# Modulation products on four column strips, two pairs' exponent bounds on the other engine, and an update rate without its sigmoid

## The chip, the cores and the metric

The kernel runs on one core of a Trainium2 chip. The metric is device time in microseconds of one execution; of several runs the median is taken. A profiled execution gives the trace from which all durations below come.

## The reference, cut to what matters

Two transformer layers work on 256 context tokens and 512 latent tokens of width 1024. The first layer's mixer is a gated delta rule ("GDN") with 8 key heads and 16 value heads, run forwards and backwards over the tokens; the second is a retention. The change touches only the beginning of the first layer.

```python
ml = [m[:, None, :] for m in adaln(c, w_mod[i], b_mod[i])]     # silu(c) @ w + b, six parts of 1024
mc = adaln(c_ctx, w_mod[i], b_mod[i])
hl = modulate(rmsnorm(xl, norm_mix_g[i]), ml[0], ml[1])        # h * (1 + scale) + shift
hc = modulate(rmsnorm(xc, norm_mix_g[i]), mc[0], mc[1])
...
# gdn_mixer
proj = jnp.concatenate([hc, hl], axis=1) @ w_in                # q, k, v, z, and ab: the gates
qkv = silu(short_conv(qkv, conv_w))
g = -jnp.exp(a_log) * softplus(ab[..., 0] + dt_bias)
beta = jax.nn.sigmoid(ab[..., 1])
...
# per head and chunk, G = cumsum(g)
seg = G[..., :, None] - G[..., None, :]
dec = jnp.where(incl, jnp.exp(jnp.where(incl, seg, 0.0)), 0.0)
a = jnp.where(strict, (k @ k.T) * dec * beta[..., :, None], 0.0)
sol = triangular_solve(a + I, rhs)                             # then the scan over chunks
```

## The kernel before, in words

The kernel is written in Python generators that emit instructions, and a scheduler that works with priorities (`tc.high_priority`) and a cost model of its own sets the order on each engine from them. Each engine then runs its instructions strictly in that written order, and so does the DMA queue of SyncE (SP in the rows), which issues nearly all loads. A change of a few instructions is therefore dealt out anew over the whole first mixer.

The start, `layer0_mix`, has three pieces that overlap.

- The modulation, `mod_cols`. Eight slices `mraw` of `w_mod` (1 MB each: scale and shift, four column blocks q of 256) are loaded. `cst` holds silu(c) and silu(c_ctx) as columns, 8 K-blocks of two vectors. For each slice eight products with a 128x2 stationary operand accumulate a 2x256 result `mps` (L146); each float32 product stands as two matmul records in the trace. ScalarE copies it to `mrow` (L148), two transposes turn it into columns `mtps` (L151), and VectorE adds bias and gain into `vec` (L155, L159).
- The tokens, `x_tile`. Six tiles of 128 tokens are loaded, normalised (L260, L262, L310) and transposed into `xraw` (L314, then L317 on ScalarE and L319 on VectorE).
- `mod_apply` turns `xraw` with `vec` into the two parts `xt` (a rounded high part, L172 on ScalarE, and a low part, L174 and L177 on VectorE), which all later projections read. A projection of one weight tile (`gemm_pair`, L91) is 24 products `gl` over the 512 latent tokens and 24 products `gc` over the context; its weights `raw` are split into `hl` by L56 (ScalarE) and L57 (VectorE).

Then `gdn_globals` computes the gates. The first projection is that of the ab columns (weights loaded by the eight small DMAs of L484). From its result come the update rate in rows 64 to 127 of `gb` (L510) and, through `xa`, Abs, Exp, Ln (L511 to L518), the log decay, whose running sum is made by two scans (L524, L526), stored to DRAM as `gd`, and brought back along the rows (`gtps` L542, `lbps` L550 turn them into columns). Behind it in program order come the conv projections of pair 0 (`conv_tile`: L579 on ScalarE and L582 on VectorE, then Silu L592, L595).

Heads are worked on in eight pairs. `gdn_bt(p)` loads the running sum along rows, broadcast to 128 partitions, as `e` (L645; 12 blocks of 128 for each direction), makes from each block relu(G_c - e), which bounds the exponent (L649), and later exp of its negative with a bias (L657). `gdn_s2(p)` multiplies masks and products with these (L673, L679, L682), and then runs a forward elimination of 30 steps on VectorE in which each step is a product `tmp` (L717) and a sum into `u` (L720) that the next step reads. After that the inverse is finished by small matmuls `ivps` (L754 and on) once VectorE has transposed the blocks (L745, L747), and the scan over chunks (`kk`, `uo`) begins. Between all this, projections of later pairs and gate tiles `zs` (L442) fill TensorE.

Of the kernel before, what the change touches and what calls it, by code (L numbers as in the profile page):

```python
# [10 lines left out]
F32 = mybir.dt.float32  # L11
# [31 lines left out]
class Trunk:  # L43
# [91 lines left out]
    def mod_cols(self, mp, pps, tags, col, xr):  # L135
        nc = self.nc
        vec = mp.tile([128, 2, 8, 2], F32, name="vec")
        for q in range(4):
            for ch in (1, 0):
                raw = mp.tile([128, 8, 256], F32, tag="mraw", name="mraw", bufs=4)  # L140
                c0 = ch * D + q * 256
                nc.sync.dma_start(
                    out=raw, in_=self.i["w_mod"][0, :, c0:c0 + 256].rearrange("(k p) f -> p k f", p=128))
                pr = pps.tile([2, 256], F32, tag=tags[ch], name="mps")
                for k in range(8):
                    nc.tensor.matmul(pr, lhsT=self.cst[:, k:16:8], rhs=raw[:, k], start=(k == 0), stop=(k == 7))  # L146
                row = mp.tile([2, 256], F32, tag="mrow", name="mrow", bufs=2)
                nc.scalar.activation(out=row, in_=pr, func=AF.Copy)  # L148
                ps = pps.tile([128, 2, 2], F32, tag="pp", name="mtps")
                for j in range(2):  # L150
                    nc.tensor.transpose(ps[:, j], row[:, j * 128:(j + 1) * 128], self.ident[0:2, 0:2])  # L151
                for j in range(2):
                    k = 2 * q + j
                    if ch:
                        nc.vector.tensor_scalar(  # L155
                            out=vec[:, 1, k], in0=ps[:, j], scalar1=col[:, 1, k:k + 1], scalar2=col[:, 2, k:k + 1],
                            op0=ALU.add, op1=ALU.mult)
                    else:
                        nc.vector.tensor_scalar(  # L159
                            out=vec[:, 0, k], in0=ps[:, j], scalar1=col[:, 0, k:k + 1], scalar2=None, op0=ALU.add)  # L160
                yield
            if q:
                self.mod_apply(vec, q - 1, xr)
# [125 lines left out]
    def layer0_mix(self):  # L289
# [58 lines left out]
        for _ in s1[0]:  # L348
            pass
        self.gdn_bt(0, st[0], prep)  # L350
        n = 0
        while True:
            with hi():
                if next(s2[0], 0) == 0:
# [3 lines left out]
                    self.gdn_kn(1, st[0], psk, scan)  # L358
                    self.gdn_bt(1, st[1], prep)
                    break  # L360
# [84 lines left out]
    def gdn_globals(self, keep, psk):  # L445
# [12 lines left out]
        with ExitStack() as es:  # L458
# [50 lines left out]
            for ps, t0, n in segs:  # L509
                nc.scalar.activation(out=gb[64:128, t0:t0 + n], in_=ps[64:128], func=AF.Sigmoid)  # L510
                nc.vector.tensor_scalar(  # L511
# [6 lines left out]
            nc.vector.scalar_tensor_tensor(out=xa, in0=xa, scalar=0.0, in1=e, op0=ALU.max, op1=ALU.add)  # L518
            nc.vector.tensor_scalar(out=xa[0:64], in0=xa[0:64], scalar1=na, scalar2=None, op0=ALU.mult)
            cm = gp.tile([64, T], F32, name="cm")  # L520
            nc.vector.memset(cm, 1.0)
# [109 lines left out]

    def gdn_bt(self, p, st, prep):
        nc = self.nc
# [8 lines left out]
        for d in range(2):  # L642
            e = prep.tile([128, 2 * NCH, CH], F32, tag=f"e{d}", name=f"e{d}")
            for h in range(2):
# [3 lines left out]
                for c in range(NCH):  # L648
                    nc.scalar.activation(  # L649
                        out=e[:, h * NCH + c], in_=e[:, h * NCH + c], func=AF.Relu, scale=-1.0,  # L650
                        bias=self.gs[:, d, 2 * p + h, c:c + 1])
            bt.append(e)
        for d in range(2):
            e = bt[d]
            for h in range(2):
                for c in range(NCH):
                    nc.scalar.activation(  # L657
                        out=e[:, h * NCH + c], in_=e[:, h * NCH + c], func=AF.Exp, scale=-1.0,
                        bias=lw[:, d, h, c:c + 1])
# [718 lines left out]
```

## Time and profile before

| | us |
|---|---|
| median of 3 runs | 2585.04 |
| lowest and highest | 2581.28, 2586.94 |
| the profiled execution | 2573.84 |
| its span in the trace | 2572.1 |
| TensorE busy in the span | 2431.1 (95%) |
| VectorE, ScalarE, GpSimd busy | 1667.7, 1073.5, 221.7 |

The profiled execution ran 11.2 us below the median, so sums are made against 2573.84 and then set on the median. TensorE is busy nearly throughout; the places where it is not are in the first mixer, which lasts until about 930 us. In the rows PE is TensorE's matmuls, PEld its weight loads, DVE VectorE, ACT ScalarE, POOL GpSimd, SPq the queue of SyncE. In brackets stands how long an engine was idle ahead of a row and what ended that.

### The profile page before, as it was taken

How to read it: one execution, taken by the hardware profiler on the slowest of the kernel's cores; microseconds unless marked ns; L12 is line 12 of the kernel's file. 1: busy time of each engine (PE TensorE's matmuls, PEld its weight loads, DVE VectorE, ACT ScalarE, POOL GpSimd, SP SyncE). 2: the span in 40 equal slices, each digit the busy share in tenths (PEclk: the TensorE clock that was granted, in tenths of full speed). 3: DMA queues.
4: the chain of work that ended last, by engine and by line, in shares of the span. 5: the costliest groups of instructions: out<-in, count | busy, mean ns of one | idle time of the engine just before them, and what ended most of it. 6: DMA issues, size and time to landing. Idle time of an engine off the chain costs nothing.

```text
span 2572.1 us, 39043 instructions
## 1 busy us (share of the span) xinstructions
PE 2431.1 (95%) x14879; PEld 2008.7 (78%) x14879; DVE 1667.7 (65%) x3362; ACT 1073.5 (42%) x2357; POOL 221.7 (9%) x268
## 2 busy tenths in 40 slices
PE   8799798998898999999999998999999999999998
PEld 4687686786777788778888887878888887788887
DVE  5568767787776755887776668874353546644446
ACT  5575555574555553253222221653231322532222
POOL 1102111111101110200000002000000002000001
PEclk9899899999899999999999999999999999999999
DMA  6332423423232247354443444243132223432332
GB/s 214 89 96 73 110 63 97 113 72 101 69 87 72 73 145 229 122 180 127 139 143 119 130 132 124 84 134 94 50 83 61 78 66 113 148 100 90 107 90 90
DMA packets 346827, 276.94 MB, mean 108 GB/s; under 512 B 105608, under 2 KB 293488, under 8 KB 346640
## 3 DMA queue, kind: packets, MB, share of 16 engines
q1 hardware_dynamic: 345616, 271.30, 35.4%
q10 hardware_dynamic: 1024, 3.15, 0.5%
q8 instruction: 117, 1.92, 0.3%
q14 instruction: 70, 0.57, 0.1%
HBM read 241.72 MB, written 32.67 MB: 107 GB/s over the span
## 4 chain that ended last, share of the span: by engine, by line
PE 55%; DVE 7%; DMA 3%; issue 2%; ACT 2%; POOL 0%; SPq 0%; POOLq 0%; ACTq 0%; DVEq 0%
PE pn L940 21%; PE gl L91 13%; PE rvp L1257 5%; PE gc L91 3%; PE rl L91 3%; PE rgp L1257 3%; PE pv L1287 2%; PE sc L1265 1%; DVE hl L57 1%; DVE ma L199 1%; PE rc L91 1%; DMA mraw<-in_w_mod 1%; ACT hl L56 0%; DVE o0acc L976 0%; DMA raw<-in_gdn_w_out 0%
## 5 line engine op out<-in xcount | busy, mean ns | idle before, releaser
L91 PE MATMUL gl<-xt,hl 128*128 128x512 f32 (+2 forms) x2760 | 700.8, 403 | 51.7 <-DVE acc L582 31.6
L91 PEld LDWEIGHTS gl<-xt,hl 128*128 128x128 f32 x2760 | 514.9, 193 | 160.0 <-issue 27.3
L57 DVE TENSOR_TENSOR hl<-raw,hl 128x1024 fp32r<-128x1024 f32 (+1 forms) x306 | 329.2, 1078 | 226.7 <-ACT hl L56 225.6
L940 PE MATMUL pn<-hl,fh 128*128 128x512 f32 x1920 | 445.0, 391 | 2.0 <-DVE fh L1074 1.9
L56 ACT ACTIVATE hl<-raw 128x1024 fp32r<-128x1024 f32 (+1 forms) x306 | 280.1, 920 | 396.9 <-PE pn L940 263.0
L940 PEld LDWEIGHTS pn<-hl,fh 128*128 128x128 f32 x1920 | 357.1, 188 | 80.1 <-DVE fh L1074 5.1
L91 PE MATMUL gc<-xt,hl 128*128 128x256 f32 x1944 | 274.8, 290 | 9.4 <-DVE acc L582 4.7
L91 PEld LDWEIGHTS gc<-xt,hl 128*128 128x128 f32 x1944 | 254.4, 194 | 20.6 <-ACT zs L442 5.4
L199 DVE SCALAR_TENSOR_TENSOR ma<-mraw,cst,ma 128x256 f32<-128x256 f32 x280 | 127.6, 496 | 40.0 <-DMA mraw<-in_w_mod 37.7
L940 PE MATMUL pn<-hl,yh 128*128 128x512 f32 x576 | 137.4, 397 | 5.4 <-DVE yh L57 4.1
L954 DVE TENSOR_TENSOR facc<-pn,facc 128x512 f32<-128x512 f32 x120 | 82.5, 689 | 83.1 <-PE pn L940 82.7
L1257 PE MATMUL rvp<-hl,xt 128*128 128x512 f32 x576 | 133.3, 390 | 0.6 <-DVE hl L57 0.6
L940 PEld LDWEIGHTS pn<-hl,yh 128*128 128x128 f32 x576 | 108.4, 191 | 31.2 <-DVE yh L57 5.8
L1257 PEld LDWEIGHTS rvp<-hl,xt 128*128 128x128 f32 x576 | 107.7, 188 | 23.5 <-DVE hl L57 1.1
L1071 ACT ACTIVATE fr<-gl 128x512 f32<-128x512 f32 x64 | 38.2, 597 | 202.1 <-PE gl L91 202.1
L582 DVE SCALAR_TENSOR_TENSOR acc<-gl,cw,acc 128x511 f32<-128x511 f32 (+1 forms) x96 | 71.5, 745 | 39.3 <-ACT acc L579 38.5
L977 POOL TENSOR_TENSOR facc<-facc,rx 128x1024 f32<-128x1024 f32 x10 | 26.5, 2645 | 781.1 <-DVE facc L976 478.8
L940 PE MATMUL pn<-hl,ryt 128*128 128x512 f32 x384 | 91.7, 396 | 0.0
L1257 PE MATMUL rgp<-hl,xt 128*128 128x512 f32 x384 | 91.3, 393 | 0.0
L91 PE MATMUL rl<-xt,hl 128*128 128x512 f32 x384 | 89.5, 391 | 0.4 <-DVE hl L57 0.4
L717 DVE TENSOR_TENSOR tmp<-u 112x30 f32<-112x30 f32 (+14 forms) x240 | 81.3, 339 | 9.2 <-POOL u L709 6.0
L940 PEld LDWEIGHTS pn<-hl,ryt 128*128 128x128 f32 x384 | 71.5, 187 | 17.0
(282 smaller groups left out, 3437.0 us busy)
## 6 DMA issues: line engine op xcount, KB each, us to landing
raw<-in_w_ff SPq DMA_DIRECT2D x128, 512.0 KB
mraw<-in_w_mod SPq DMA_DIRECT2D x112, 256.0 KB
raw<-in_gdn_w_in SPq DMA_DIRECT2D x96, 256.0 KB
raw<-in_ret_w_in SPq DMA_DIRECT2D x32, 512.0 KB
mraw<-in_w_mod SPq DMA_DIRECT2D x24, 512.0 KB
e<-gd SPq DMA_DIRECT2D x32, 384.0 KB
mraw<-in_w_mod SPq DMA_DIRECT2D x8, 1024.0 KB
raw<-in_gdn_w_out SPq DMA_DIRECT2D x16, 512.0 KB
```

Of the source, the lines that this page charges most:

```text
L56: nc.scalar.activation(out=hi, in_=src, func=AF.Copy)
L57: nc.vector.tensor_tensor(out=lo, in0=src, in1=hi.bitcast(F32), op=ALU.subtract)
L91: nc.tensor.matmul(ps, lhsT=w(a, k), rhs=xt[:, b, k, t0:t0 + n], start=(k == 0 and i == 0), stop=(k == 7 and i == 2))
L199: eng.scalar_tensor_tensor(out=accs[v], in0=raw[:, k], scalar=c, in1=accs[v], op0=ALU.mult, op1=ALU.add)
L582: nc.vector.scalar_tensor_tensor(out=acc[:, t0 + a:t0 + a + m], in0=ps[:, b:b + m], scalar=c[j], in1=acc[:, t0 + a:t0 + a + m], op0=ALU.mu ...
L717: nc.vector.tensor_tensor(out=t3, in0=u3[:, 0:c, c:c + 1].to_broadcast([112, c, n]), in1=u3[:, c:c + 1, c + 1:32].to_broadcast([112, c, n] ...
L940: m = nc.tensor.matmul(ps, lhsT=lhs(a, k, t), rhs=hls[hf][k // 2][:, b, k % 2], start=(k == 0 and n == 0), stop=(k == 3 and n == 2))
L954: nc.vector.tensor_tensor(out=dst, in0=ps, in1=dst, op=ALU.add)
L977: nc.gpsimd.tensor_tensor(out=a, in0=a, in1=x, op=ALU.add)
L1071: nc.scalar.activation(out=r, in_=ps, func=AF.Relu)
L1257: nc.tensor.matmul(ps, lhsT=xt[:, a, kk, t * 128:(t + 1) * 128], rhs=hls[kk // 2][:, b, kk % 2], start=(kk == 0 and n == 0), stop=(kk == 7 ...
L1287: nc.tensor.matmul(pvs[it], lhsT=pts[jt][:, i, it * 128:(it + 1) * 128], rhs=v[:, j, jt], start=(jt == 0 and n == 0), stop=(jt == 5 and n ...
```

## The change

Three things are changed. First, the eight modulation products of a slice go to four strips of 32 columns of the array: the stationary operand becomes `c32`, the two vectors padded with zeros to 32 columns, K-block k goes to strip k mod 4, and each strip adds up two K-blocks. The result then has four partial sums on 128 partitions, and the two transposes become two products with `sel`, a 128x2 matrix with ones at rows 0, 32, 64, 96 (and 1, 33, 65, 97), which turn and add up in one. Second, for pairs 0 and 1 the 24 bounds of `gdn_bt` are made on VectorE, as min(e - G_c, 0), and the exponential takes scale 1 there. Third, the update rate is exp(-softplus(-b)), taken from the softplus that the log needs anyway, in one activation after the Ln, in place of two sigmoids ahead of `xa`.

```diff
     def mod_cols(self, mp, pps, tags, col, xr):
+        c32 = mp.tile([128, 8, 32], F32, name="c32")
+        sel = mp.tile([128, 2], F32, name="sel")
+        nc.vector.memset(c32, 0.0)
+        nc.vector.tensor_copy(c32[:, :, 0:2], self.cst.rearrange("p (v k) -> p k v", v=2))
+        nc.vector.tensor_copy(sel, self.ident[:, 0:2])
+        for g in (32, 64, 96):
+            nc.vector.tensor_tensor(out=sel, in0=sel, in1=self.ident[:, g:g + 2], op=ALU.add)
...
-                pr = pps.tile([2, 256], F32, tag=tags[ch], name="mps")
+                pr = pps.tile([128, 256], F32, tag=tags[ch], name="mps")
                 for k in range(8):
-                    nc.tensor.matmul(pr, lhsT=self.cst[:, k:16:8], rhs=raw[:, k], start=(k == 0), stop=(k == 7))
-                row = mp.tile([2, 256], F32, tag="mrow", name="mrow", bufs=2)
+                    g = 32 * (k % 4)
+                    nc.tensor.matmul(
+                        pr[g:g + 32], lhsT=c32[:, k], rhs=raw[:, k], start=(k < 4), stop=(k >= 4),
+                        tile_position=(0, g))
+                row = mp.tile([128, 256], F32, tag="mrow", name="mrow", bufs=2)
                 nc.scalar.activation(out=row, in_=pr, func=AF.Copy)
                 ps = pps.tile([128, 2, 2], F32, tag="pp", name="mtps")
                 for j in range(2):
-                    nc.tensor.transpose(ps[:, j], row[:, j * 128:(j + 1) * 128], self.ident[0:2, 0:2])
+                    nc.tensor.matmul(
+                        ps[:, j], lhsT=row[:, j * 128:(j + 1) * 128], rhs=sel, start=True, stop=True)
...
-        self.gdn_bt(0, st[0], prep)
+        self.gdn_bt(0, st[0], prep, True)
...
-                    self.gdn_bt(1, st[1], prep)
+                    self.gdn_bt(1, st[1], prep, True)
...
             for ps, t0, n in segs:
-                nc.scalar.activation(out=gb[64:128, t0:t0 + n], in_=ps[64:128], func=AF.Sigmoid)
...
             nc.vector.tensor_scalar(out=xa[0:64], in0=xa[0:64], scalar1=na, scalar2=None, op0=ALU.mult)
+            nc.scalar.activation(out=gb[64:128], in_=xa[64:128], func=AF.Exp, scale=-1.0)
...
-    def gdn_bt(self, p, st, prep):
+    def gdn_bt(self, p, st, prep, dve=False):
...
                 for c in range(NCH):
-                    nc.scalar.activation(
-                        out=e[:, h * NCH + c], in_=e[:, h * NCH + c], func=AF.Relu, scale=-1.0,
-                        bias=self.gs[:, d, 2 * p + h, c:c + 1])
+                    g = self.gs[:, d, 2 * p + h, c:c + 1]
+                    t = e[:, h * NCH + c]
+                    if dve:
+                        nc.vector.tensor_scalar(
+                            out=t, in0=t, scalar1=g, scalar2=0.0, op0=ALU.subtract, op1=ALU.min)
+                    else:
+                        nc.scalar.activation(out=t, in_=t, func=AF.Relu, scale=-1.0, bias=g)
...
                     nc.scalar.activation(
-                        out=e[:, h * NCH + c], in_=e[:, h * NCH + c], func=AF.Exp, scale=-1.0,
+                        out=e[:, h * NCH + c], in_=e[:, h * NCH + c], func=AF.Exp, scale=1.0 if dve else -1.0,
                         bias=lw[:, d, h, c:c + 1])
```

The scheduler deals the order anew. Three places show it.

TensorE at the end of the modulation and in the first projection, before. `mps` are the modulation products, `mtps` the turns, `gl` and `gc` the first projection, and `cwps` turns the conv weights:

```order
L151 MATMUL mtps<-ident,mrow 128x2 x2
L146 MATMUL mps<-mraw,cst 2x256 x6
L91 MATMUL gl<-xt,hl 128x512 x3
L151 MATMUL mtps<-ident,mrow 128x2 x2
L91 MATMUL gl<-xt,hl 128x512 x3
L463 MATMUL cwps<-ident,cwr 128x128
L91 MATMUL gl<-xt,hl 128x512 x16
```

The same place in the changed kernel (lines further down are shifted by 11, here L463 to L474):

```order
L161 MATMUL mtps<-sel,mrow 128x2 x2
L154 MATMUL mps<-mraw,c_116 32x256 x8
L161 MATMUL mtps<-sel,mrow 128x2 x2
L474 MATMUL cwps<-ident,cwr 128x128
L91 MATMUL gl<-xt,hl 128x512 x2
L91 MATMUL gc<-xt,hl 128x256 x2
L91 MATMUL gl<-xt,hl 128x512 x22
```

The first projection stood between the last modulation slice and its turn, and now stands behind both.

ScalarE in the chain of the gates, from the exponential of `a_log` (`na`) to the Ln, before:

```order
L503 ACTIVATE na<-na 64x1
L56 ACTIVATE hl<-raw 128x512
L510 ACT_TABLE_LOAD
L510 ACTIVATE gb<-gl 64x512
L56 ACTIVATE hl<-raw 128x512
L510 ACTIVATE gb<-gc 64x256
L514 ACTIVATE e<-xa 128x768
L56 ACTIVATE hl<-raw 128x512
L515 ACT_TABLE_LOAD
L515 ACTIVATE e<-e 128x768
L517 ACT_TABLE_LOAD
L517 ACTIVATE e<-e 128x768
```

And now (L514 is the old L503, L524 the old L514, L530 the new exponential):

```order
L514 ACTIVATE na<-na 64x1
L56 ACTIVATE hl<-raw 128x512 x3
L524 ACTIVATE e<-xa 128x768
L525 ACTIVATE e<-e 128x768
L527 ACT_TABLE_LOAD
L527 ACTIVATE e<-e 128x768
L530 ACT_TABLE_LOAD
L530 ACTIVATE gb<-xa 64x768
```

Of the two table loads ahead of the first Exp of `e` none is left; a weight split that stood between Abs and Exp has moved ahead.

VectorE at the beginning of pair 0's elimination, before:

```order
L717 TENSOR_TENSOR tmp<-u 112x30
L57 TENSOR_TENSOR hl<-raw,hl 128x512
L720 TENSOR_TENSOR u<-u,tmp 112x30
L582 SCALAR_TENSOR_TENSOR acc<-gc,cw,acc 128x255
L717 TENSOR_TENSOR tmp<-u 112x58
L720 TENSOR_TENSOR u<-u,tmp 112x29x2
L717 TENSOR_TENSOR tmp<-u 112x84
L720 TENSOR_TENSOR u<-u,tmp 112x28x3
```

And now, where `e_1880` is pair 1's tile of bounds:

```order
L732 TENSOR_TENSOR tmp<-u 112x30
L57 TENSOR_TENSOR hl<-raw,hl 128x512
L735 TENSOR_TENSOR u<-u,tmp 112x30
L593 SCALAR_TENSOR_TENSOR acc<-gc,cw,acc 128x255
L732 TENSOR_TENSOR tmp<-u 112x58
L663 TENSOR_SCALAR e_1880<-e_1880,gs 128x128
L735 TENSOR_TENSOR u<-u,tmp 112x29x2
L663 TENSOR_SCALAR e_1880<-e_1880,gs 128x128
L732 TENSOR_TENSOR tmp<-u 112x84
```

The 24 bounds of pair 1 now stand one by one between the elimination's dependent steps, all ahead of its last eight steps.

## The prediction

> **What bounds the kernel now.** First I read the page's shares: TensorE is busy 95% of the span, so time can be won only where TensorE waits, or where what it does itself is the path. Next the stretches, to find these places. Columns: stretch, its length, busy time of PE, PEld, DVE, ACT, POOL with instruction counts, granted TensorE clock, DMA share, GB/s. The last line is from the waits of the load queue: total, times, longest.
>
> ```profile
> 16.00:20.00 4.00, 4.00 (x24) 1.90 (x23) 1.38 (x3) 2.38 (x5) 0.46 (x1) 1.00 1.07 396
> 20.00:24.00 4.00, 4.00 (x23) 1.94 (x22) 2.89 (x8) 2.25 (x5) 0.64 (x2) 1.00 0.76 238
> 34.00:35.00 1.00, 1.00 (x6) 0.42 (x5) 0.96 (x2) 1.00 (x2) 0.01 (x1) 1.00 1.11 363
> 35.00:36.00 1.00, 1.00 (x7) 0.32 (x4) 1.00 (x3) 0.66 (x2) 0.00 (x0) 1.00 0.94 144
> 30.00:46.00 16.00, 16.00 (x82) 6.63 (x80) 13.88 (x37) 9.50 (x17) 0.73 (x2) 1.00 0.54 141
> 200.00:930.00 730.00, 653.35 (x6029) 544.09 (x6029) 545.24 (x1429) 418.10 (x1208) 113.46 (x161) 0.96 0.31 83
> ...
> SPq L308 <- DVE njunk L310: 10.5, 3, 3.9
> ```
>
> The modulation slices arrive at nearly 400 GB/s until about 35.4 us (the rate falls to 144 in the last of these microseconds). From 30 to 46 us TensorE is busy without a break while the DMA has run dry: there the modulation products themselves are the path. The lull from 20 to 24 us is worth (396 - 238)/396 x 4 = 1.6 us of transfer; the token loads L308 waited then for buffers that the normalisation on VectorE frees, and that stood behind TensorE's products.
>
> Then the timeline, for the end of the modulation and the first projection. Columns: start, duration, engine, line, operation; in brackets the idle time ahead of it.
>
> ```profile
> 36.07 3.62 PE L146 MATMUL mps<-mraw,cst 128*2 128x256 f32 x16
> 43.58 2.75 PE L146 MATMUL mps<-mraw,cst 128*2 128x256 f32 x12
> 44.39 0.69 DVE L57 TENSOR_TENSOR hl<-raw,hl 128x512 fp32r<-128x512 f32 x1
> 46.43 0.37 ACT L148 ACTIVATE mrow<-mps 2x256 f32<-2x256 f32 x1 [1.85 <-PE mps L146]
> 47.16 0.28 PE L151 MATMUL mtps<-ident,mrow 2*128 2x2 f32 x2
> 47.47 0.35 DVE L159 TENSOR_SCALAR vec<-mtps,col 128x2 f32<-128x2 f32 x2 [0.93 <-PE mtps L151]
> 47.73 2.51 ACT L172 ACTIVATE xt<-xraw,vec 128x512 fp32r<-128x512 f32 x4 [0.93 <-DVE vec L159]
> 51.36 0.96 DVE L177 TENSOR_TENSOR xt<-xraw,xt 128x768 fp32r<-128x768 f32 x1
> 52.94 2.56 PE L91 MATMUL gc<-xt,hl 128*128 128x256 f32 x20
> ```
>
> The last slice's products end at 43.58 + 2.75 = 46.33, eleven microseconds after its data; `vec` follows at 47.82, the last low part of `xt` at 52.32, and the ab projection ends at 55.50. That is the anchor of the sum.
>
> **Term 1, the strips: -3.7 us.** The trace has the same form elsewhere: `mod_rows` makes eight products on four strips, 128 columns wide.
>
> ```profile
> 260.76 0.62 PE L232 MATMUL mps<-mraw,cst 128*2 128x128 f32 x16
> 55.33 5.63 PE L91 MATMUL gl<-xt,hl 128*128 128x512 f32 x24
> 70.74 6.70 PE L91 MATMUL gl<-xt,hl 128*128 128x512 f32 x24
> 64.00:68.00 4.00, 1.16 (x11) 0.96 (x9) 3.94 (x5) 2.27 (x3) 0.00 (x0) 0.76 0.07 12
> 68.00:72.00 4.00, 3.52 (x12) 2.49 (x13) 3.73 (x17) 0.36 (x1) 0.00 (x0) 0.50 0.17 39
> ```
>
> At 256 columns I estimate a slice at 2 x 0.62 = 1.24 us against 3.62, so TensorE sheds 8 x 2.4 = 19 us. Most of that is not gained, since the data now sets the time. Step by step: with TensorE out of the tokens' way the lull should go, and the last slice lands at 34.0 instead of 35.4; products until 35.5 (0.3 for the start); the way from products to `vec` stays 47.82 - 46.33 = 1.5, so 37.0; from `vec` to the last low part it was 52.32 - 47.82 = 4.5, and VectorE now has a pending L177 and a cast on the way, some 0.6 more: 42.1. The weight split L57, which stood before `vec`, is now behind this: 0.69, so 42.8. Then 22 `gl` at 5.63/24 and 22 `gc` at 2.56/20 make 5.2 + 2.8 = 8.0: 50.8. TensorE has been idle since 37, though. After the idle stretch at 64 to 68 us the granted clock was 0.76 and then 0.50, and the 24 `gl` that followed took 6.70 instead of 5.63; I add that difference, 1.1. The projection ends at 51.8 instead of 55.5.
>
> The Trainium skill, "TensorE: Matmul & The Clock Gate", section on the HAM clock gate, says that an idle window of about 3.4 us puts the array at half rate until it has been busy for as long; by that the cold start would lose an estimated 1.7 us instead of 1.1 and the whole sum would be -4.6 instead of -5.2. The row at 68 us agrees with the half rate (0.50); the length it does not settle. The same rule lets the thinned-out slices before 34 us run cold, which the data hides.
>
> Bounds: with no lull recovered and twice the clock loss the end is 54.3 (-1.2); with 33.8 and a warm clock 50.5 (-5.0). I take the middle since each half has a row. The setup of `c32` and `sel` is six small VectorE instructions of at most a few tenths, ahead of data that arrives after 7 us; the copy `mrow` keeps its 256 elements per partition. Both cost nothing here; uncovered, the setup would cost about a microsecond, once.
>
> **Term 2, the gates: -2.7 us.**
>
> ```profile
> 55.53 0.38 ACT L510 ACTIVATE gb<-gc 64x256 f32<-64x256 f32 x1 [0.70 <-PE gc L91]
> 55.95 0.54 DVE L511 TENSOR_SCALAR xa<-gc,sgn,dtb 128x256 f32<-128x256 f32 x1 [0.32 <-ACT gb L510]
> 56.53 0.85 ACT L514 ACTIVATE e<-xa 128x768 f32<-128x768 f32 x1 [0.61 <-DVE xa L511]
> 59.20 0.85 ACT L515 ACTIVATE e<-e 128x768 f32<-128x768 f32 x1
> 62.24 0.96 DVE L518 SCALAR_TENSOR_TENSOR xa<-xa,e 128x768 f32<-128x768 f32 x1 [1.60 <-ACT e L517]
> 63.77 0.60 DVE L519 TENSOR_SCALAR xa<-xa,na 64x768 f32<-64x768 f32 x1
> 66.19 1.75 DVE L526 TENSOR_TENSOR_SCAN gb<-cm,xa 32x768 f32<-32x768 f32 x1
> 67.99 0.90 PE L542 MATMUL gtps<-ident,gb 128*128 128x128 f32 x3 [2.84 <-DVE gb L526]
> ```
>
> From 55.50 to the end of the second scan at 67.94 TensorE has only a projection to fill with and runs dry (2.84 us). Away go: the sigmoid ahead of `xa`, about 0.35; the table load and the split between Abs (end 57.38) and Exp (59.20), 1.8; the conv sum between L518 (end 63.20) and L519, 0.57, which the new order puts behind the scans. Added is one exponential, about the 0.85 of its neighbours, with a table load; it lies beside L519 and two scans of 1.75 each and is done before them. Without this cover it would hold `gtps` up by some 2 us. Bounds -1.5 (a split falls back between) to -2.8.
>
> **Terms 3 and 4, the bounds on VectorE: 0 and +1.2 us.**
>
> ```profile
> L649 ACT ACTIVATE e<-e,gs 128x128 f32<-128x128 f32 x192 | 60.5, 391 | 3.8 <-DMA e<-gd 3.8
> L1195 DVE TENSOR_SCALAR dp<-dl 128x224 f32<-128x224 f32 x4 | 1.1, 274 | 0.1
> L174 DVE TENSOR_SCALAR xraw<-xraw,vec 128x256 f32<-128x256 f32 x8 | 3.1, 409 | 0.0
> 73.89 1.87 ACT L649 ACTIVATE e<-e,gs 128x128 f32<-128x128 f32 x6 [2.34 <-DMA e<-gd]
> 138.67 0.39 DVE L717 TENSOR_TENSOR tmp<-u 112x228 f32<-112x228 f32 x1
> 138.97 0.69 DVE L57 TENSOR_TENSOR hl<-raw,hl 128x512 fp32r<-128x512 f32 x1
> 139.57 0.39 DVE L720 TENSOR_TENSOR u<-u,tmp 112x228 f32<-112x228 f32 x1
> 142.24 0.41 DVE L717 TENSOR_TENSOR tmp<-u 112x240 f32<-112x240 f32 x1
> 142.68 0.41 DVE L720 TENSOR_TENSOR u<-u,tmp 112x240 f32<-112x240 f32 x1
> 166.91 0.57 DVE L745 STREAM_TRANSPOSE v<-tt 32x384 f32<-32x384 f32 x1 [0.29 <-DMA tt<-vd]
> 168.44 0.24 PE L754 MATMUL ivps<-v,off 32*32 32x32 f32 x2
> ```
>
> A pair's 24 bounds leave ScalarE (24 x 1.87/6 = 7.5 us) and come to VectorE at about 0.2 to 0.27 each, 5 to 6.5 us. For pair 0 they wait there for the broadcast `e`, as ScalarE did (2.34 us), and behind them now stand the conv sums of the second projection. These need its `gl`, which ended at 70.74 + 6.70 = 77.4, 3.5 us after `e` came; so the wait and half the work lie beside TensorE, and the other half is about what the sums no longer wait for ScalarE. I take 0, bounds -1.5 and +1.5; with the cover gone it costs 5.
>
> For pair 1 they stand inside pair 0's elimination, whose every step reads the one before. A step takes 0.44 (142.24 to 142.68), with a 0.69 split put in 0.90 (138.67 to 139.57): an inserted instruction costs its duration less 0.23. At 274 ns, the nearest row, that is 0.05 x 24 = 1.2 us; at 409 ns it is 4.3. I take the first, whose operation and width are nearer. The lower bound is 0, since the first `ivps` started 1.0 us after its `v` (167.48). The 7.5 us that ScalarE sheds there give nothing: it waited for `gl`.
>
> **The sum.** -3.7 - 2.7 + 0 + 1.2 = -5.2 us: the profiled execution of 2573.84 becomes 2568.6, and on the median of 2585.04 that is 2579.8. All of it must hold through 200 to 930 us, where TensorE is idle 730 - 653 = 77 us, and whose order is dealt anew. 0.2%, about what a measurement of this kernel can tell from no change, is 5.2 us: the forecast lies on that edge.
>
> **Rivals.**
> - The new order spends the filler at the wrong places. Each pair's inverse needs projections to fill TensorE; if more of them are used up inside the scan, the 77 us of idle time grow. For it: rows are shuffled among all pairs; against: the projections per pair are nearly as many as before. An eighth more idle time is +9.6, so 2589.4; from 5.2 us on it eats the gain, from 10.4 us on the kernel is slower. Chance 0.17.
> - The same shuffle fills better, and a sixth of the idle time goes: another -8 to -13, about 2570. Chance 0.15.
> - The start is hidden by its transfers anyway: the lull stays, the ab weights (small, slow loads behind the last slice) and the cold clock hold the projection, the gates win 2 and pair 1 loses 2: about 2584. For it: after 36 us the DMA moves only such loads. Chance 0.10.
> - The forecast, 0.58, of which 0.35 beyond the edge and 0.23 within; its own range is 2575.7 to 2583 (worst ends +3.1, best -9.3, hardly all at once).
>
> Faster by over 0.2%: 0.35 + 0.15 = 0.50; within: 0.23 + 0.10 = 0.33; slower 0.17. The range, 2567 to 2591, reaches into both shuffle cases.
>
> **What would show it.** Term 1: a slice's products in about 1.2 us, the ab `gc` ending near 52. Term 2: no ScalarE table load between Abs and Exp, and 12.4 - 2.7 = 9.7 us from the end of `gc` to that of the second scan. Terms 3 and 4: bounds of 0.2 to 0.3 us, the elimination hardly longer than before, the first `ivps` some 5 us earlier. The prediction fails if the first mixer's end moves by more or less than the start did: then the order, not the three edits, has set the time.

## The result: 0.84% slower, and the profile after

| | before | changed |
|---|---|---|
| median (6 runs each, us) | 2583.63 | 2604.29 |
| lowest, highest | 2578.61, 2586.94 | 2601.71, 2610.66 |
| profiled execution | 2573.84 | 2601.71 |

The ratio is 1.0084, 95% interval 1.0068 to 1.01. Forecast was 2579.8 (2567 to 2591). The two profiled executions differ by 27.9 us, the medians by 20.7, since that of before was some 10 us below its median.

Where the 27.9 us arose is read from three stretches, cut at the end of pair 0's exponentials (L657) and at the first product of the next stage, `pn`. First before, then the changed kernel; the columns are those of the stretches shown with the prediction.

```profile
0.00:102.10 102.10, 84.49 (x434) 55.63 (x434) 55.57 (x130) 63.62 (x127) 14.78 (x26) 0.95 0.52 163
102.10:958.00 855.90, 769.41 (x6972) 643.44 (x6973) 624.66 (x1597) 492.02 (x1362) 124.81 (x178) 0.96 0.33 89
958.00:2572.10 1614.10, 1577.21 (x7475) 1309.58 (x7474) 987.48 (x1637) 517.89 (x868) 82.13 (x64) 0.99 0.37 114
```

```profile
0.00:112.70 112.70, 81.26 (x450) 61.05 (x450) 62.29 (x160) 54.59 (x100) 14.19 (x26) 0.81 0.49 147
112.70:985.30 872.60, 786.33 (x6973) 655.94 (x6974) 627.17 (x1621) 484.55 (x1339) 127.17 (x178) 0.94 0.32 87
985.30:2600.00 1614.70, 1577.96 (x7475) 1309.97 (x7473) 988.08 (x1637) 517.63 (x868) 81.98 (x64) 0.99 0.37 114
```

The start lost 10.6 us, the rest of the first mixer 16.7, what follows 0.6. In the middle stretch TensorE runs the same 6972 products and is idle as long (86.5 and 86.3 us), but it is busy 16.9 us longer: the products themselves ran slower. The granted clock of the stretch fell with them, from 0.96 to 0.94.

The start, on TensorE in the changed kernel:

```profile
30.49 1.93 PE L154 MATMUL mps<-mraw,c 128*32 128x256 f32 x16
...
36.67 1.94 PE L325 MATMUL nps<-ident,njunk 128*128 128x128 f32 x8 [0.68 <-DVE njunk L321]
...
41.51 1.07 PE L154 MATMUL mps<-mraw,c 128*32 128x256 f32 x16
...
44.30 1.93 PE L154 MATMUL mps<-mraw,c 128*32 128x256 f32 x16
47.05 1.01 PE L161 MATMUL mtps<-sel,mrow 128*128 128x2 f32 x4 [0.82 <-ACT mrow L158]
48.00 1.93 PE L154 MATMUL mps<-mraw,c 128*32 128x256 f32 x16
...
57.13 6.95 PE L91 MATMUL gl<-xt,hl 128*128 128x512 f32 x22 [0.60 <-DVE hl L57]
63.91 2.80 PE L91 MATMUL gc<-xt,hl 128*128 128x256 f32 x22
```

A slice's products take 1.93 us and only once 1.07; eight token transposes mostly take 1.94. Before, the same eight took

```profile
18.01 1.10 PE L314 MATMUL nps<-ident,njunk 128*128 128x128 f32 x8
```

Below, "cold" stands for these longer durations of equal rows. Each turn stands ahead of the next slice and waits for ScalarE's copy, so that the last two slices follow each other after 3.7 us, as before (3.75). And they begin late. The load queue, before and then changed:

```profile
16.69 4.58 SPq L308 DMA_DIRECT2D x<-in_x  x2
21.38 8.03 SPq L142 DMA_DIRECT2D mraw<-in_w_mod  x4
```

```profile
19.06 7.44 SPq L319 DMA_DIRECT2D x<-in_x  x2
26.61 6.29 SPq L149 DMA_DIRECT2D mraw<-in_w_mod  x4
```

The last two token loads wait longer for their buffers, and the last four slices behind them are issued 5.2 us later. They also move more slowly, at 348 instead of 382 GB/s in full stretches, before and then changed (0.50 in the second is the granted clock):

```profile
28.00:32.00 4.00, 4.00 (x26) 2.30 (x25) 2.15 (x5) 1.94 (x5) 0.49 (x1) 1.00 1.09 382
```

```profile
32.00:36.00 4.00, 3.38 (x16) 2.50 (x12) 2.14 (x7) 2.75 (x7) 1.10 (x2) 0.50 1.09 348
```

The gates, on ScalarE and VectorE in the changed kernel:

```profile
67.32 0.85 ACT L524 ACTIVATE e<-xa 128x768 f32<-128x768 f32 x1
68.20 0.85 ACT L525 ACTIVATE e<-e 128x768 f32<-128x768 f32 x1
...
72.52 0.84 ACT L530 ACTIVATE gb<-xa 64x768 f32<-64x768 f32 x1
```

```profile
74.66 1.75 DVE L537 TENSOR_TENSOR_SCAN gb<-cm,xa 32x768 f32<-32x768 f32 x1
```

Exp follows Abs at once, the new exponential ends before the second scan, and from the end of `gc` (66.71) to that of the scan (76.41) it is 9.7 us, as forecast.

Little of this is left at the end of the start. From the end of the ab `gc` to that of pair 0's exponentials the changed kernel takes 46.0 us, before took 46.6, and the change without its strips (e4 below) 43.5. Behind the gates the changed kernel's products are still cold. Pair 0's 24 `gl`, changed and then in e4:

```profile
81.35 7.24 PE L91 MATMUL gl<-xt,hl 128*128 128x512 f32 x24 [1.39 <-DVE acc L593]
```

```profile
70.05 5.69 PE L91 MATMUL gl<-xt,hl 128*128 128x512 f32 x24 [1.39 <-DVE acc L582]
```

### The profile page after: what moved, and what is told of

Its sections match the earlier page's. It is cut to its first block, busy times and chain, and to the rows that moved or that the text cites. A ratio compares the mean times of both kernels' runs of the same rounds, so it can differ in the third digit from the quotient of the medians.

```text
span 2600.0 us, 39088 instructions
## 1 busy us (share of the span) xinstructions
PE 2445.5 (94%) x14895; PEld 2027.0 (78%) x14895; DVE 1677.5 (65%) x3416; ACT 1056.8 (41%) x2306; POOL 223.3 (9%) x268
## 4 chain that ended last, share of the span: by engine, by line
PE 59%; DVE 7%; DMA 2%; ACT 2%; issue 2%; POOL 1%; SPq 0%; POOLq 0%; ACTq 0%; DVEq 0%
PE pn L955 22%; PE gl L91 13%; PE rvp L1272 5%; PE gc L91 4%; PE rl L91 3%; PE rgp L1272 3%; PE pv L1302 2%; PE sc L1280 1%; DVE hl L57 1%; PE rc L91 1%; DVE ma L210 1%; PE kk L890 1%; PE uo L880 0%; ACT hl L56 0%; DVE o0acc L991 0%
## 5 line engine op out<-in xcount | busy, mean ns | idle before, releaser
L91 PE MATMUL gl<-xt,hl 128*128 128x512 f32 (+2 forms) x2760 | 710.3, 407 | 53.8 <-DVE acc L593 30.8
L91 PEld LDWEIGHTS gl<-xt,hl 128*128 128x128 f32 x2760 | 521.6, 196 | 164.9 <-issue 25.2
L57 DVE TENSOR_TENSOR hl<-raw,hl 128x1024 fp32r<-128x1024 f32 (+1 forms) x306 | 328.6, 1076 | 235.1 <-ACT hl L56 234.0
```

What stands on the lines that cost most here:

```text
L57: nc.vector.tensor_tensor(out=lo, in0=src, in1=hi.bitcast(F32), op=ALU.subtract)
L91: nc.tensor.matmul(ps, lhsT=w(a, k), rhs=xt[:, b, k, t0:t0 + n], start=(k == 0 and i == 0), stop=(k == 7 and i == 2))
```

## The experiments

Each was timed beside before. The ab end is that of the ab `gc`; the way is the middle stretch, from the end of pair 0's exponentials to the first `pn`. In the profiles with a star the third and fourth token loads wait 10.1 to 10.4 us instead of 7.4 to 7.7. The one kernel that was profiled both ways (e16 with, e18 without) ends its ab projection 2.2 us later with that wait. For kernels with strips there is no such pair, so their times are compared as they stand.

| run | median, us | before | ratio, 95% interval | ab end | start ends | way |
|---|---|---|---|---|---|---|
| before (profile above) | | | | 55.5 | 102.1 | 855.9 |
| changed | 2604.29 | 2583.63 | 1.0084 (1.0068, 1.01) | 66.7 | 112.7 | 872.6 |
| e1 strips | 2596.43 | 2585.8 | 1.005 (1.0033, 1.0067) | 68.7 | 115.4 | 856.3 |
| e2 gates | 2583.73 | 2585.8 | 0.9992 (0.9978, 1.0006) | 57.8* | 102.6 | 856.1 |
| e3 bounds | 2600.67 | 2585.8 | 1.0061 (1.0044, 1.0077) | 57.8* | 101.8 | 873.4 |
| e4 gates, bounds | 2596.46 | 2585.8 | 1.0051 (1.0034, 1.0068) | 55.7 | 99.2 | 873.7 |
| e8 17 bounds | 2581.26 | 2580.67 | 1.0006 (0.9992, 1.0021) | 57.8* | 104.7 | 859.6 |
| e10 18 bounds | 2603.7 | 2579.78 | 1.0071 (1.0051, 1.009) | 55.9 | 102.9 | 874.9 |
| e5 strips, products added | 2587.55 | 2580.67 | 1.0023 (1.0013, 1.0033) | 63.4* | 109.8 | 860.3 |
| e6 strips, order | 2595.1 | 2580.67 | 1.0051 (1.0032, 1.0069) | 70.2* | 117.4 | 860.3 |
| e7 strips, both | 2582.44 | 2580.67 | 1.0002 (0.9991, 1.0014) | 57.9* | 104.7 | 858.9 |
| e9 sel 64 bytes | 2591.2 | 2579.78 | 1.0039 (1.0024, 1.0053) | 66.0 | 112.4 | 859.6 |
| e13 sel 512 bytes | 2599.02 | 2585.27 | 1.0058 (1.004, 1.0075) | 66.8 | 113.8 | 860.2 |
| e11 strips repaired | 2582.51 | 2579.78 | 1.0002 (0.9991, 1.0014) | 62.3* | 109.1 | 856.6 |
| e12 the same, gates | 2581.27 | 2579.78 | 0.9993 (0.9979, 1.0006) | 63.3 | 107.5 | 855.7 |
| e14 all repairs, gates | 2581.5 | 2585.27 | 0.9988 (0.9974, 1.0002) | 57.4 | 99.6 | 858.7 |
| e15 and early ab | 2582.89 | 2580.51 | 1.0002 (0.9989, 1.0015) | 56.4 | 100.9 | 857.5 |
| e16 gates, early ab | 2575.34 | 2580.51 | 0.9975 (0.9964, 0.9986) | 58.4* | 100.8 | 858.6 |
| e17 early ab | 2579.06 | 2579.36 | 0.9998 (0.9987, 1.001) | 56.9 | 103.1 | 857.2 |
| e18 = e16 again | 2575.32 | 2579.36 | 0.9985 (0.9976, 0.9994) | 56.2 | 98.6 | 856.6 |

**The parts alone.** e1 is before with the change's `mod_cols`; e2 and e3 are these lines, and e4 both:

```diff
-                nc.scalar.activation(out=gb[64:128, t0:t0 + n], in_=ps[64:128], func=AF.Sigmoid)
+            nc.scalar.activation(out=gb[64:128], in_=xa[64:128], func=AF.Exp, scale=-1.0)
```

```diff
-        self.gdn_bt(0, st[0], prep)
+        self.gdn_bt(0, st[0], prep, True)
-                    self.gdn_bt(1, st[1], prep)
+                    self.gdn_bt(1, st[1], prep, True)
```

> Only the four strips with the selection product; gates and bounds as before. Theory A (the start is lost to the strips: a slice's eight products run at the cold clock in about 1.9 us, the token loads are issued later, and the last slice lands late): the ab projection ends near 66 us instead of 55.5, the gate chain stays 12.4 us, and the start loses about 11 us by the end of pair 0's exponentials. Theory B (what happens behind that point is the newly dealt order, not an edit): the way from there to the first product of the next stage (855.9 us before, 872.6 in the changed kernel) comes out at some third value between 850 and 880. Total by both: +5 to +30. Rival C (strips are sound, the late start came from the gates' or the bounds' instructions standing ahead): the ab projection ends at 56 or earlier and the total is at most +2.

> Only the update rate from the softplus. Theories A and B: the ab projection ends near 55.5 as before, the chain from there to the end of the second scan takes 9.7 instead of 12.4 us, the end of pair 0's exponentials comes 2 to 3 us earlier, and the rest moves by anything within 15 us, either way. Rival D (the rest follows the content: each edit's own effect is carried through unchanged): total -2 to -3 us with the later way at 855 to 857.

> Only the bounds of pairs 0 and 1 on VectorE. Theories A and B: start as before up to the gates, pair 0's elimination about 2 us longer (33.9 before, 35.8 in the changed kernel), the rest anything within 15 us. Rival E (the bounds among the dependent steps of the elimination are what the changed kernel loses behind the start): the elimination grows by 2 and the way from pair 0's exponentials to the next stage by 10 to 17, total +10 to +17.

> The changed kernel without its strips. Theory A: the start wins the gates' 2 to 3 us, total within 15 us either way (theory B: the order is dealt anew). Rival D: the two single results add up. Rival E: +8 to +15.

The strips lose 13.3 us at the start and nothing behind it; the bounds lose 17.5 us of the way and nothing at the start. In e2 and e4 it is 10.2 us from the end of `gc` to that of the second scan, not the 9.7 expected: there a weight split still stands between Exp and Ln. Medians add up: strips +10.6 and gates with bounds +10.7 make 21.3, the change cost 20.7. Theory A holds. Theory B falls in its first form: strips and gates leave the order of all later pairs as it was (TensorE's order differs from before's only up to 64 us with the strips and up to 93 us with the gates), and the way with it. Only the bounds deal it anew. Rival E has the right sum, so content and order had to be separated.

**One bound more or less.** A kernel with n of pair 1's 24 bounds on VectorE keeps before's order of the later pairs at n = 17, and has another from pair 1 on at n = 18:

```diff
-                    if dve:
+                    if d * 12 + h * 6 + c < int(dve):
...
-                    self.gdn_bt(1, st[1], prep)
+                    self.gdn_bt(1, st[1], prep, 17)
```

> The kernel before with 17 of the 24 bounds of pair 1 on VectorE and none of pair 0. With 17, TensorE's order differs from before's in a few rows at the beginning only, and all later pairs keep their order; with 18 and with 24 the whole first mixer is dealt anew. Theory B' (the loss behind the start is the newly dealt order of pairs 2 to 7, in which TensorE does the same products at a lower clock): the first product of the next stage comes within 2 us of before, and the total is within 0.2%. Rival E (the bounds themselves, on a VectorE that the elimination waits for): 17/24 of the +17.2 us of all bounds, +12, and already in pair 0's elimination.

> The kernel before with 18 of the 24 bounds of pair 1 on VectorE, one more than the run with 17, whose order behind the start stayed as before; with 18 the order of pairs 1 to 6 is dealt anew. Theory B' (the deal of the order sets the time, through the clock): the way from the end of pair 0's exponentials to the next stage differs from that with 17 (859.6) by several us, in either direction, and TensorE's busy time there differs at equal work. Rival (cost of a bound): within 1 us of the run with 17.

The middle stretch with 17, then with 18:

```profile
104.70:964.30 859.60, 774.09 (x6973) 647.70 (x6974) 626.15 (x1614) 487.53 (x1345) 125.30 (x178) 0.95 0.33 89
```

```profile
102.90:977.80 874.90, 784.67 (x6973) 655.72 (x6974) 626.85 (x1615) 485.96 (x1344) 125.22 (x178) 0.95 0.32 87
```

One bound more comes with 15.3 us, of which 10.6 are longer busy time at equal work and 4.7 idle time. A bound itself takes 0.28 us, so it is the order. (17 bounds cost 3.7 of way, not the 2 expected; 3.2 of it is in pair 0's elimination.) How an order can make products slower is seen in pair 1's inverse. Before, where a whole `gc` projection stands between its small products, and then e3:

```profile
280.29 4.99 PE L91 MATMUL gc<-xt,hl 128*128 128x256 f32 x24
285.21 0.92 PE L784 MATMUL ivps<-v,off 64*64 64x64 f32 x24
```

```profile
266.13 2.05 PE L91 MATMUL gc<-xt,hl 128*128 128x256 f32 x15
...
268.28 1.33 PE L91 MATMUL gc<-xt,hl 128*128 128x256 f32 x9
...
278.43 1.55 PE L788 MATMUL ivps<-v,off 64*64 64x64 f32 x24 [1.42 <-DVE tt L780]
```

In e3 the projection is spent ahead of the inverse, and the 64x64 products between the waits take 1.55 instead of 0.92 us. Over the whole way these products (L788), with 17 and then with 18 bounds:

```profile
L788 PE MATMUL ivps<-v,off 64*64 64x64 f32 x384 | 14.9, 222 | 1.9 <-DVE tt L780 0.9 <-ACT v L768 0.7
```

```profile
L788 PE MATMUL ivps<-v,off 64*64 64x64 f32 x384 | 20.1, 242 | 4.7 <-DVE tt L780 3.5 <-issue 0.6 <-ACT pc L794 0.6
```

That is 5.2 of the 10.6 us; `gl` and `gc` grow by 2.9 and 2.1. In e3 it is another row that grows most. Over the whole way the 1080 `gl`, before and in e3:

```profile
L91 PE MATMUL gl<-xt,hl 128*128 128x512 f32 x1080 | 310.2, 423 | 45.7 <-DVE acc L582 28.7 <-DVE hl L57 6.8 <-ACT zs L442 5.4
```

```profile
L91 PE MATMUL gl<-xt,hl 128*128 128x512 f32 x1080 | 319.6, 434 | 41.6 <-DVE acc L582 28.1 <-ACT zs L442 5.8 <-ACT hl L56 3.7
```

That is 9.4 of the 18.2 us by which busy time grew (787.63 against 769.41), with less idle time ahead of them. So that the order alone can cost 15 us is shown; which products lengthen differs from order to order, and why these `gl` did is not shown.

**Clock and order at the start.** e5 adds products to the strips, e6 forces before's order, e7 does both and adds eight products behind the last slice (the added results are used nowhere):

```diff
+                dm = pps.tile([2, 256], F32, tag="py", name="dm")
+                for k in range(3):
+                    nc.tensor.matmul(dm, lhsT=self.cst[:, k:16:8], rhs=raw[:, k], start=(k == 0), stop=(k == 2))
```

```diff
+            with self.tc.issue_after(self.sq):      # the newest token square; also around L172 and the copy of x_tile
                 nc.scalar.activation(out=row, in_=pr, func=AF.Copy)
...
+            with self.tc.issue_after(mm):           # the last product of the next slice
                 for j in range(2):
                     nc.tensor.matmul(ps[:, j], ...)
```

> The strips alone, with three extra products of the old form (128x2 stationary operand, result unused, 3 x 0.45 us) behind each slice's eight: more work on TensorE, otherwise the order of the strips alone but for the second token tile's square, which now stands ahead of the first tile's copy. Theory W (in the strips kernel TensorE is too thinly occupied, its clock drops and products, transposes and turns take nearly twice as long): slices fall from 1.93 to about 1.1 us, eight transposes from 1.94 to 1.1, and the ab projection ends at 57 to 60 us instead of 68.7. Theory O (it is the order: token squares behind copies, so that the loads of the last four slices are issued at 27 instead of 21.4 us, and each turn ahead of the next slice): it stays at 65 or later, since the extra products only add. Before: 55.5.

> The strips alone, with the order of the kernel before forced on ScalarE (each token tile's square ahead of the copies of the tile before and of the modulation rows) and each slice's turn put behind the next slice's products on TensorE; no extra work. Theory O: the loads of the last four slices are issued at about 21 us, the last slice lands at 35, and the ab projection ends at 55 to 59 us instead of 68.7. Theory W: slices and transposes still run at 1.9 us, TensorE's own chain stays behind the data, and the ab projection ends at 60 or later.

> The forced order and the three extra products for each slice, and eight more behind the last slice. If W and O both hold, the ab projection ends at 51 to 54 us, which is what the forecast had for the strips (51.8), and the total is 2 to 4 us below before. If it ends at 55 or later, something else holds the start, the landing of the data (35.4 us in the kernel before) first of all.

e5, the same place as above, with more work on TensorE:

```profile
40.47 1.07 PE L154 MATMUL mps<-mraw,c 128*32 128x256 f32 x16
41.35 1.46 PE L159 MATMUL dm<-mraw,cst 128*2 128x256 f32 x6
42.74 0.61 PE L164 MATMUL mtps<-sel,mrow 128*128 128x2 f32 x4
43.28 1.07 PE L154 MATMUL mps<-mraw,c 128*32 128x256 f32 x16
```

With 24 products added five of the eight slices take 1.07 instead of 1.93 us, the last turns 0.61 instead of 1.01, and the ab end comes 5.3 us earlier: theory W is shown by the durations of equal rows, but its 57 to 60 us are not reached (63.4). Order alone wins nothing (e6: 70.2, slices still at 1.93, the last four issued at 29.2), so theory O falls as a cause of its own. Yet the order counts once the array is not cold. With the products added, the forced order wins another 5.5 us (e5 to e7, which also has the eight products behind the last slice); with the order forced, the products win 12.3 (e6 to e7). Together they give 57.9: of the 13.2 us lost, 10.8 are back, but not the 51 to 54 that were expected. The projection's 22 `gl`, 7.06 us long in e1, are then no longer cold:

```profile
49.95 5.32 PE L91 MATMUL gl<-xt,hl 128*128 128x512 f32 x22 [1.93 <-DVE hl L57]
```

**The loads.** All kernels with strips up to here move their slices at 348 to 369 GB/s. The buffers `mraw` begin behind `c32` and `sel`: at a multiple of 512 bytes in each partition before, 32 bytes beyond one in the change, 64 beyond in e9, at a multiple again in e13. The order in e9 and e13 is e1's.

```diff
-        sel = mp.tile([128, 2], F32, name="sel")
+        sel = mp.tile([128, 128], F32, name="sel")[:, 0:2]      # e13; [128, 16] in e9
```

> The strips alone, with sel laid out in 64 instead of 8 bytes for each partition (its first two columns are used), which moves the buffers mraw behind it by 32 bytes; the order on every engine is that of the strips alone. All five kernels with strips moved their slices at 348 to 369 GB/s, all five without at 380 to 400, and the mean packet of 1 KB took 49 to 51 instead of 46 ns. Theory P (the buffers lie off a 64 byte boundary through sel, and a packet takes longer to write): 46 ns again and 380 GB/s or more in the full stretches, the ab projection 2 to 3 us earlier than the strips alone (68.7), total 2 to 3 us less. Rival (the strips' reads on TensorE or the longer copies slow the loads): 49 to 51 ns and 348 GB/s stay.

> The strips alone again with the order of the strips alone, and sel laid out in 512 bytes for each partition: the buffers mraw then begin at a multiple of 512 bytes within the partition, as in the kernel before; in the changed kernel they begin 32 bytes beyond one, in the run with sel in 64 bytes 64 beyond one. Theory P2 (packets of 1 KB that begin off a multiple of 512 bytes take 46 to 60 instead of 46 ns to land): packets of 46 ns, 380 GB/s or more in the full stretches, the ab projection at 64 to 67 us instead of 68.7. Rival (it isn't where the buffers lie, but TensorE's faster reading or the copies): 49 ns and 348 GB/s again.

e1, then e13:

```profile
8.00:12.00 4.00, 1.73 (x16) 0.45 (x8) 1.20 (x2) 1.42 (x3) 1.64 (x3) 1.00 1.08 367
12.00:16.00 4.00, 2.91 (x16) 2.52 (x20) 2.10 (x4) 0.16 (x1) 3.67 (x3) 1.00 1.07 362
```

```profile
8.00:12.00 4.00, 1.44 (x16) 0.36 (x8) 1.46 (x2) 1.42 (x3) 1.89 (x3) 1.00 1.07 397
12.00:16.00 4.00, 3.16 (x20) 2.60 (x24) 1.85 (x4) 0.41 (x1) 3.42 (x3) 1.00 1.08 404
```

In e9 it stays at 367 and 361. The mean over the 8192 packets of 1 KB that make up the slices, worked out from the trace's packets, is 50.9 ns in e1 and 50.6 in e9, but 46.8 in e13 and 46.6 before. P falls, P2 holds. What faster loads are worth is not shown: e13's ab end comes 1.9 us earlier than e1's, but e9's, with the slow packets, 2.7 earlier, and by their ratios neither can be told from e1. The Trainium skill, "DMA: Bandwidth & Descriptors", section "How a descriptor splits into AXI transactions", says that a transaction must start at a multiple of 256 bytes, so that a descriptor that starts beside one also pays for bytes in front of it that are not used. It speaks of what is read; here it is the place written that moved, and no run shows that the rule holds for it. An estimate from that page, 33 or 34 beats for 32, would be 3 or 6%; the packets took 8 to 9% longer.

**Are repaired strips worth anything?** e11 has order, added products (six behind the last turn) and the 64 bytes, e12 the gates too; e14 has the 512 bytes and three behind the last turn; e15 none there, but the ab weights early, by this edit, and e16 to e18 that edit without strips:

```diff
-            segs = self.gemm_pair(self.w_cols(load_ab))
+            with self.tc.high_priority(100):
+                wab = self.w_cols(load_ab)
+            segs = self.gemm_pair(wab)
```

> The strips alone with all three repairs: the forced order, three extra products for each slice but none behind the last, six behind the last turn, and sel padded. If the three causes (clock, order, buffers off their boundary) are what the start lost, the slices land at 380 GB/s, a slice takes 1.07 us, and the ab projection ends at 51 to 54 us; total 1 to 4 us below before. If it ends at 55 or later, VectorE's chain behind vec (L174, L177, L57), which ran without a gap from 35 to 51 us in the run with order and extra products, is the next bound and the strips are worth nothing here.

> The repaired strips with the gates' new update rate, and all bounds on ScalarE as before: the candidate for a kernel faster than both. By the parts: gates -2 to -3, repaired strips 0 to -4; total 2 to 7 us below before (2574 to 2582 on a median of before near 2581 to 2586). If the later pairs absorb the gain, within 1 us of before.

> All repairs and the gates: forced order, three extra products behind every slice and three behind the last turn (eight before, six in the other candidate, where they held up the turn of the conv weights and with it VectorE), sel in 512 bytes, update rate from the softplus, all bounds on ScalarE. If P2 holds the slices land 3 us earlier than in the run with order and extra products (ab projection 57.9 there), ab projection at 53 to 56 us, gates 9.7 to 10.5 us, total 3 to 6 us below before. If not, 0 to 3 us below.

> As the last candidate (forced order, three extra products behind each slice, sel in 512 bytes, gates' new rate), without the extra products behind the last turn, and with the loads and splits of the ab weights moved ahead by priority, so that the ab projection's own products stand between the last slices and turns. In the last candidate the 22 gl waited 2.91 us for the split hl and ran at the low clock (6.89 us instead of 5.2). If that was the rest of the start, the ab projection ends at 47 to 53 us instead of 57.4 and the total is 5 to 10 us below before. If the small loads of the ab weights, each about 0.8 us of the load queue, now stand in the slices' way, the last slices land 2 to 3 us later and the end is 53 or later.

> The control without strips: the old modulation products, the gates' new rate and the early loads of the ab weights. The products still end at 46 us, so the ab projection ends at 53 to 55.5. Difference to the run before in this list = what repaired strips are worth: by the forecast's own reasoning 3 to 5 us at the ab projection; if they are worth nothing, the two end alike.

> The kernel before with the early loads of the ab weights alone, old gates, old products. The control of the last run (gates and early loads, 6.4 us below before by the medians of that run, though its profile's first projection ended no earlier): if the early loads carry the gain, it is here again, 4 to 6 us below before; if the gates carry it, 0 to 3 us; if it was the second layer, where some executions of each kernel wait 7.0 us longer behind ro (rtp, near 2170 us) and that kernel's did not, the runs spread over 8 us or more again and the median lies within 3 us of before.

> The run with gates and early loads once more, unchanged: a ratio between 0.996 and 0.9985 if its gain is of the kernel; 0.9985 to 1.001 if it was of that run.

In e11 and e12 the products behind the last turn cost time: they stood ahead of the turn of the conv weights, for which VectorE waited 3.2 us. In e14 the last `vec` is done at 44.6, 3.3 us earlier than before (47.82), and yet the ab end comes at 57.4, since there the next limits show:

```profile
44.35 0.22 DVE L161 TENSOR_SCALAR vec<-mtps,col 128x2 f32<-128x2 f32 x1
47.85 6.89 PE L91 MATMUL gl<-xt,hl 128*128 128x512 f32 x22 [2.91 <-DVE hl L57]
```

VectorE's casts and splits (before's L174, L177 and L57), without a long gap from 35 to 49 us, hold the products up, and these are cold again. In e15 the projection fills the gaps, but the small ab loads stand between the slices, and the seventh slice's products start at 40.6 instead of 35.7 us; besides, its scans wait for `lbps`, so that it is 11.8 instead of 9.7 us from the end of `gc` to that of the second scan.

No kernel with repaired strips can be told from before by its median, though three of the four have the gates too, and none has its ab end ahead of before's 55.5. e15 and e16, timed side by side, differ in the repaired strips alone: e15's start ends at 100.9, e16's at 100.8* (98.6 in its repetition e18), and e15 is 7.5 us slower by the medians. So no gain of the strips could be shown in four attempts.

e16, without strips, and its repetition e18 are the only kernel faster than before in the whole interval, by 0.25 and 0.15% (2575.3 both times); the second ratio, 0.9985, lies on the border that was set for it. Early ab alone is worth nothing that can be told (e17), and neither are the gates alone (e2). In e18's profile the start ends 3.5 us earlier than before's and the first `pn` comes 2.8 earlier; behind `pn`, however, this profile takes 5.7 us longer than before's, so it does not show where the gain of the medians comes from. Part of the medians is of another kind: profiles of e2, e15 and others have a wait of 7.0 us in the second layer,

```profile
2175.21 1.12 PE L1316 MATMUL rtp<-ident,ro 128*128 128x128 f32 x4 [6.98 <-DVE ro L1313]
```

and those of before, e16, e17 and e18 have not. Why it comes, how often, and how much of the gain of e16 and of the difference to e15 is due to it, stays open.

## Why the prediction was wrong

- **Term 1 is the step that failed** (-3.7; measured +10.6 for the start of the change, +13.3 for the strips alone). Its number for a slice, 1.24 us, holds where the array is not cold (1.07), and the way from `vec` (51.9) to the ab end (66.7) is the forecast's, 14.8. All of the miss lies ahead of `vec`, which came at 51.9 instead of 37.0: the last slice landed at 42.7 (the last packet in the trace) instead of 34.0, and its products ended 7.2 us behind that (49.9) instead of 1.5. Two sentences of the term failed. One says that the slices run cold "which the data hides". The rule of the Trainium skill on the clock gate ("TensorE: Matmul & The Clock Gate", section on the HAM clock gate) was given a price for the end of the stage and none for the stage itself. Thinned out from 3.62 us, a slice took 1.93 us and not 1.07, and the token transposes, which the change does not touch, lengthened nearly as much. The data did not hide this, since the data itself came late. The other says that "the lull should go": it grew, because TensorE, cold, and the new order of squares and copies stood in the tokens' way. The last slices were issued at 26.6 instead of 21.4 us and moved at 348 instead of 382 GB/s. e5 to e7 show that time and order had both to be mended. The lower bound (-1.2) left no room for a loss.
- **Term 2 had the right size**: 9.7 us forecast, 9.7 measured in the change and also in e12, e14, e16 and e18; with the gates' edit in the old surroundings it is 10.2 (e2, e4), a gain of 2.2 and within the bounds. What failed is that the sum carries it to the end: in the change only 0.6 us of terms 2 and 3 together is left at the end of the start (46.0 against 46.6).
- **Term 3**: forecast 0, between -1.5 and +1.5. e3 and e8 both have their ab end at 57.8 and differ up to pair 0's exponentials only in pair 0's bounds: 101.8 against 104.7, so -2.9. That is better than the lower bound; that ScalarE's relief was undervalued fits, but no run separates it.
- **Term 4**: +1.2; pair 0's elimination went from 33.9 to 35.8 us, +1.9, with bounds of 0.28 us.
- **The first rival came true in kind**: the new order spends its filler at the wrong places. It had a chance of 0.17 and a price of 9.6 us from longer idle time; it cost 16.7, and idle time did not change. What grows is the time that the products take. For the 64x64 products of the inverse this goes with filler that no longer stands between them and their waits; for the rest it is not shown. The order listing showed that projections per pair were nearly the same, and that was taken as evidence against; it says nothing on where within a pair they stand.
- The sign that the prediction named for its failure, the mixer's end moving by another amount than the start, was right: +27.2 against +10.6.

## What to carry to other kernels

Making TensorE's part of a stage shorter can make the stage longer: here, with the products thinned out, the pieces on TensorE took 1.7 to 1.8 times as long as when it was kept busy, untouched work too. Ask first whether TensorE stays busy, and test with useless products before building on the gain. Where a scheduler deals the order, change one instruction at a time until the order tips; a pair of kernels on both sides of that edge separates what an edit costs from what its order costs. And look where a new small tile moves the buffers behind it.

## What was not expected of the hardware

- In e1 the granted clock stands at 1.00 from 4 to 46 us while slices take 1.93 and transposes 1.94 us; in the changed kernel the column reads 0.61 and 0.54 from 30 to 62 us at the same durations. So the column did not always show what the durations of equal rows did, and that the clock is behind them in e1 is inferred from the added products, not read.
- A buffer that begins off a multiple of 512 bytes (32 or 64 beyond) took the loads of 1 KB pieces from 380 to 404 down to 348 to 369 GB/s. An offset of 256 was not tried.
